# Full fp32 products on unsplit operands in the mixing phases of a decoder trunk

## The chip, the cores and the metric

The kernel runs on one core of one Trainium2 chip. The metric is the device time of one execution in microseconds (us); less is better. Times of two kernels are compared from runs on the same chip.

## The reference

Two layers (`DEPTH = 2`) work on 256 tokens of 1024 features in fp32. Each layer is a half-step feed-forward, a mixing part and a second half-step feed-forward. The mixing part joins two groups of heads, sparse attention and a gated linear recurrence (HGRN2):

```python
for l in range(DEPTH):
    x = x + 0.5 * swiglu(rmsnorm(x, ffn1_norm[l]), ffn1_w_gate[l], ffn1_w_up[l], ffn1_w_down[l])
    h = rmsnorm(x, mix_norm[l])
    proj = h @ w_in[l]
    (q, kc, vc, ksl, vsl, kw, vw, gts, hq, hf, hi, hg) = jnp.split(proj, offsets, axis=-1)
    ...
    o_nsa = nsa_group(...)      # 8 heads of 64, 2 key groups, three branches
    o_hg = hgrn2_group(...)     # 4 heads of 128
    x = x + jnp.concatenate([o_nsa, o_hg], axis=-1) @ w_out[l]
    x = x + 0.5 * swiglu(rmsnorm(x, ffn2_norm[l]), ffn2_w_gate[l], ffn2_w_up[l], ffn2_w_down[l])
```

In the attention each head has three softmaxes, over compressed blocks, selected blocks and a window; their outputs, weighted by gates, are added:

```python
o_s = jnp.einsum("bgrqnl,bgqnld->bqgrd", p2.astype(dt), vg)
o_w = jnp.einsum("bgrqk,bkgd->bqgrd", p3.astype(dt), vwb)
o = gb[..., 0:1] * o_c + gb[..., 1:2] * o_s + gb[..., 2:3] * o_w
```

With 256 tokens the selected blocks are all blocks and the window holds every earlier token, so both branches are causal attention over the whole sequence.

## The kernel before

The tokens stand as two halves of 128, h = 0 and 1. The weights come as a stream of units of 512 KB, in one order for the whole program, phase by phase: feed-forward, mixing, feed-forward, twice. A unit holds two K tiles of 128 rows by 512 columns. `load_stream` (L373) loads each into one of three raw buffers (`raw`, fp32); `hi_stream` (L391) rounds it to fp32r on ScalarE into `hi` of one of five ring slots; `lo_stream` (L410) subtracts, on VectorE or GpSimd, to give `lo`, and then frees the raw buffer. The activations are split in the same way (`split`, L363): a rounded part on ScalarE, the rest on VectorE. A product of two split operands is three fp32r matmuls, hi hi, hi lo and lo hi (L463 to L465; L493 to L495 where the weights are the stationary operand). `stream` (L436) issues the products of one half; a ring slot is free when both halves have used its unit.

A mixing phase has input products (`w_in`, 24 full units and 4 narrower ones), then 8 units of output weights (`w_out`) in `OUT_ORDER`: part 0 multiplies the attention's outputs for both halves of the columns, part 1 the recurrence's. Beside the stream run tasks for the attention (`attend_task`, L1082, with `head_task`, `turn_task` and `cmp_task`) and for the recurrence (`level_task`, `products`, `out_task`). `turn_task` (L1172) transposes 128 keys of four heads' probabilities into PSUM and splits them into `pth` and `ptl`; `pv` (L1118) multiplies them by the values `vh` and `vl`, which stand between columns of zeros (`pad`, L561). The attention's output is split into `ah` and `al` (L1140), the recurrence's into the activations' tiles `XH` and `XL` (L1411), which is why it waits for the end of the input products (L1409).

The order of instructions on each engine is made when the program is built: `Sched.run` (L193) takes, of all tasks, the operation that could start first by costs that the program holds for each kind of operation, plus a penalty per task (`PEN`); where several engines could run it, it takes the one that would end first. `stream_pen` (L509) holds the second half back in the last `LAG = 4` units of a phase until the first half is done, so that the first half's norm (`resid`, `norm`, `norm_turn`, L650 to L682) can run beside the second half's products. All transfers are issued by SyncE's queue, in one order.

Of the kernel before, what the change touches and what calls it, by code (L numbers as in the profile page):

```python
# [25 lines left out]
LARGE = 85.0   # the exponential of more could overflow  # L26
LEVELS = [0, 1, 2, 4, 8, 16, 32]

# columns of the constant array
# [9 lines left out]
# moving layout of the keys of a group: sel 1 | sel 0 | win 0 | win 1 | compressed  # L39
# [5 lines left out]
RING = 5       # split weight units held  # L45
RAW = 3        # unsplit weight units held
BOOT = 3       # units split by K tiles at the start
# when the rest of the inputs is loaded: after which unit of weights, half, from and to which 256 columns
BOOT_X = ((-1, 0, 1, 2), (0, 0, 2, 4), (2, 1, 0, 2), (3, 1, 2, 4))
FIRST = (-0.3, -0.4, 0.5, 1.3, 0.1, 0.6, 0.9, 0.2)  # L50
LAG = 4        # units by which the halves of the tokens are apart at a phase's ends
NBUF = 14      # general buffers of the mixing part
# [3 lines left out]
# how eager the tasks are (less: earlier)  # L56
# [43 lines left out]
class Op:  # L100
    """An instruction (or a few for one engine), with the engines that could run it, each with what it costs there."""
# [15 lines left out]
LOAD = 1.28    # a switch of ScalarE's tables  # L117
# [4 lines left out]
class Sched:  # L122
    """Emits the instructions of tasks that run side by side, in the order in which they could start.

    A task is a generator. It yields an Op (and is sent the op's end), or a request: wait for a key
    or a condition, set a key, acquire a slot (sent the slot), release it. An op waits for what its
    task has waited for or done before."""
# [26 lines left out]
    def resolve(self, t):  # L154
        """A request that isn't an op; whether it could be met."""
        what, arg = t.req[0], t.req[1]
        if what == "wait":
            if callable(arg):
                if not arg():
                    return False  # L160
            elif arg not in self.keys:
                return False
            else:
                t.deps += self.keys[arg]
            self.advance(t)
        elif what == "deps":
            t.deps = list(arg)
            self.advance(t)
        elif what == "set":
            self.keys[arg] = list(t.deps)  # L170
            self.advance(t)
        elif what == "acq":
            have = self.slots[arg]
            n = t.req[2]
            if len(have) < n:
                return False
            have.sort(key=lambda x: max((d[0] for d in x[1]), default=0.0))
            got = [have.pop(0) for _ in range(n)]
            self.last_acq = [y for _, d in got for y in d]
            t.deps += self.last_acq  # L180
            self.advance(t, [x for x, _ in got])
        elif what == "rel":
            for x in t.req[2]:
                self.slots[arg].append((x, list(t.deps)))
            self.advance(t)
        return True
# [6 lines left out]
    def run(self):  # L193
        while self.tasks:
# [29 lines left out]
            if eng == "DMA":  # L224
                # its issue, then the transfer, which others hold up
                issued = end - cost + 0.475
                self.moved = max(issued + 0.65, self.moved) + cost
                end = self.moved + 0.87
# [7 lines left out]
def four(t):  # L236
    """Two K tiles of 512 columns as four of 256."""
    return t.rearrange("p a (b n) -> p (a b) n", b=2)
# [29 lines left out]
class Block:  # L268
    """Columns of a product that share an accumulator: [128 tokens, n] for each half, or, where the weights are the
    stationary operand, [128 columns, 2, 256 tokens]."""  # L270
# [5 lines left out]
class Unit:  # L276
    """1024 x 128 of a block's weights: two K tiles of 512 columns, or four of 256."""

    def __init__(self, block, kt, srcs, first, last, act, need):
        self.block, self.kt, self.srcs = block, kt, srcs  # L280
        self.first, self.last, self.act, self.need = first, last, act, need


class Trunk(Sched):
# [33 lines left out]
    def copy(self, out, in_, after=None):  # L318
        """A copy, by either of two engines."""
# [36 lines left out]
    def transposes(self, pairs):  # L356
        """pairs: (out, in)."""
# [9 lines left out]
    def rope_norm(self, st, n):  # L367
        """st [128, 2, n]: sums of squares in, inverse norms out, both in the first row."""
# [22 lines left out]
    def hi_stream(self):  # L391
        for i, u in enumerate(self.units):
            self.at_hi = i
            if i >= BOOT:
                yield wait(("raw", i))
            (s,) = yield acq("ring")
# [13 lines left out]
    def lo_stream(self):  # L410
        for i, u in enumerate(self.units):
# [12 lines left out]
            yield wait(("hi", i))  # L424
            hi, lo = self.split_w[i]
# [10 lines left out]
    def stream(self, h):  # L436
        for p, (a, b) in enumerate(self.phases):
            self.phase_at[h] = p
            for i in range(a, b):
# [19 lines left out]
                def mm(t):  # L459
                    ah, al = u.act(h, u.kt + t)  # L460
                    st, sp = u.first and t == 0, u.last and t == 1
                    f = self.nc.tensor.matmul
                    f(ps[:, :k.n], ah, hi[:, t, :k.n], start=st, stop=False)  # L463
# [3 lines left out]
                for t in range(2):  # L467
                    if i < BOOT:
                        yield wait(("lo", i, t))
                    yield self.P(3 * (0.0025 + k.n / 2400), lambda: mm(t))  # L470
                self.used[i] = self.used.get(i, 0) + 1
                if self.used[i] == 2:
                    yield rel("ring", self.split_w.pop(i))
# [51 lines left out]
    def control(self):  # L525
        """One phase's memory after the other's."""
# [8 lines left out]
    def start(self):  # L535
# [14 lines left out]
        self.padded = [per.tile([128, 4, 320], F32R, name=n) for n in ("vh", "vl")]  # L550
# [10 lines left out]
    def pad(self):  # L561
        """Zeros that stay, of what only in part takes data."""
        nc = self.nc
        vh, vl, gv, vcb = self.padded
        for t in [gv, vcb] + self.pcs:
            yield self.G(0.25, lambda: nc.gpsimd.memset(t, 0.0))
        z = vcb[:, 0:1, 0, :64].to_broadcast([128, 4, 64])
        for v in (vh, vl):
            for o in (0, 128, 256):
                yield self.G(0.97, lambda: nc.gpsimd.tensor_copy(v[:, :, o:o + 64], z))  # L570
        yield put("padded")

    def boot(self):
        """What the start waits for, in the order in which it is needed."""
# [34 lines left out]
    def first_turn(self, h, n):  # L609
        """The first product starts before the norm is known: of the inputs times the gains, transposed."""  # L610
# [47 lines left out]
    def norm(self, h, i):  # L658
        """The i-th norm of the half h: its transposed, split activations."""
# [179 lines left out]
    def mix(self, l):  # L839
# [3 lines left out]
        M = {}  # L843
# [65 lines left out]
        def values(h, br, src):  # L909
            """src [128, g, 64] -> split, between columns of zeros."""  # L910
            c = lambda v: v[:, 2 * br + h, 64:].rearrange("p (g d) -> p g d", g=2)[:, :, :64]
            yield from self.split(c(M["vh"]), c(M["vl"]), src)
# [169 lines left out]
        def attend_task(h, g):  # L1082
# [3 lines left out]
            # the heads' segments: branch, where in the scores, width, mask  # L1086
# [21 lines left out]
            vh, vl, vcb = M["vh"], M["vl"], M["vcb"]  # L1108
# [4 lines left out]
            for i, (so, vi) in enumerate(tiles):  # L1113
                yield wait(key("pt", h, g, i))
                yield wait(key("v", vi % 2, vi // 2))
                th, tl = M["pt", h, g, i]

                def pv(e):  # L1118
                    o = 64 + 128 * g - 64 * e
                    c = slice(256 * e, 256 * e + 256)  # L1120
                    f = nc.tensor.matmul
                    f(po[:, :256], vh[:, vi, o:o + 128], th[:, c], start=(i == 0 and e == 0), stop=False)
                    f(po[:, :256], vl[:, vi, o:o + 128], th[:, c], start=False, stop=False)
                    f(po[:, :256], vh[:, vi, o:o + 128], tl[:, c], start=False, stop=False)

                for e in range(2):
                    yield P(0.33, lambda: pv(e))
                yield rel("pth", (th, tl))
# [11 lines left out]
            yield from self.split(M["ah", h][:, s], M["al", h][:, s], po[:, :256].rearrange("p (k t) -> p k t", k=2))  # L1140
# [3 lines left out]
        def head_task(h, g, r, part, pr, mx):  # L1144
            """One head's probabilities, weighted by the gates of their branches."""
# [26 lines left out]
        def turn_task(h, g, i, so, pr):  # L1172
            (pt,) = yield acq("short")
            yield self.transposes([(pt[:, 128 * k:128 * k + 128], pr[r][:, so:so + 128]) for k, r in enumerate((0, 2, 1, 3))])
            ((th, tl),) = yield acq("pth")
            yield from self.split(th, tl, pt)
            M["pt", h, g, i] = th, tl
# [3 lines left out]
        def cmp_task(h, g):  # L1181
            """The probabilities of the compressed branch, transposed."""
# [40 lines left out]
        def f_task(c, ps):  # L1223
            """The forget gates of two heads, transposed."""
# [101 lines left out]
        def products(h, i, a, b, x):  # L1326
            """A level's products within 64 tokens: for its right halves alone, but for the diagonal."""
# [28 lines left out]
        def last_product(h, x):  # L1356
# [9 lines left out]
            # what is no longer needed holds the whole matrix  # L1366
# [11 lines left out]
        def out_task(h):  # L1378
# [30 lines left out]
            yield wait(lambda: self.phase_done_in(h))  # L1409
            c = slice(128 * h, 128 * h + 128)  # L1410
            yield from self.split(self.XH[:, 4:8, c], self.XL[:, 4:8, c], h4(pt))  # L1411
# [18 lines left out]
        act = lambda h, kt: self.xact(h, kt) if kt > 3 else (M["ah", h][:, kt], M["al", h][:, kt])  # L1430
        for ni, (part, n) in enumerate(OUT_ORDER):
            for k in (2 * part, 2 * part + 1):
# [3 lines left out]
                us.append(Unit(bs[n], 2 * k, [(wo[256 * k:256 * k + 256, 512 * n:512 * n + 512], 0)], first, last, act, need))  # L1436

        def opened(pool, p):
# [3 lines left out]
            self.slots["hx"] = [(T([128, 512], f"hx{i}"), []) for i in range(4)]  # L1442
            self.slots["pth"] = [((T([128, 512], f"pth{i}", F32R), T([128, 512], f"ptl{i}", F32R)), []) for i in range(2)]
# [8 lines left out]
            for h in range(2):  # L1452
                M["ah", h], M["al", h] = T([128, 4, 128], f"ah{h}", F32R), T([128, 4, 128], f"al{h}", F32R)
# [11 lines left out]
            M["vh"], M["vl"], M["gv"], M["vcb"] = self.padded  # L1465
# [64 lines left out]
```

## Time and profile before

| what | value |
|---|---|
| median of 3 runs | 1146.16 us (1146.1 to 1149.26) |
| span of the profiled execution | 1147.0 us; the page gives no other time of it |
| TensorE (PE) busy | 1080.8 us, 94% |
| VectorE (DVE) busy | 720.7 us, 63% |
| ScalarE (ACT) busy | 571.7 us, 50% |
| GpSimd (POOL) busy | 200.5 us, 17% |
| mean granted TensorE clock | 0.976 |
| the chain that ended last | PE 75%, DVE 16%, issue 4%, DMA 2% |

The busy shares are means over the whole span. The feed-forwards make up most of it, and TensorE is busy there almost throughout; the mixing phases lie at about 211 to 391 us and 773 to 954 us and look different, so they are read by stretches. PEld is the load of stationary operands and runs beside PE. A matmul's duration holds its latency; what the engine needs for one is the step from its start to the next one's start.

### The profile page before, as it was taken

How to read it: one execution, taken by the hardware profiler on the slowest of the kernel's cores; microseconds unless marked ns; L12 is line 12 of the kernel's file. 1: busy time of each engine (PE TensorE's matmuls, PEld its weight loads, DVE VectorE, ACT ScalarE, POOL GpSimd, SP SyncE). 2: the span in 40 equal slices, each digit the busy share in tenths (PEclk: the TensorE clock that was granted, in tenths of full speed). 3: DMA queues.
4: the chain of work that ended last, by engine and by line, in shares of the span. 5: the costliest groups of instructions: out<-in, count | busy, mean ns of one | idle time of the engine just before them, and what ended most of it. 6: DMA issues, size and time to landing. Idle time of an engine off the chain costs nothing.

```text
span 1147.0 us, 18786 instructions
## 1 busy us (share of the span) xinstructions
PE 1080.8 (94%) x7420; PEld 974.6 (85%) x7420; DVE 720.7 (63%) x1187; ACT 571.7 (50%) x899; POOL 200.5 (17%) x193
## 2 busy tenths in 40 slices
PE   5999999988879999999999999999898799999998
PEld 4999988777668799998879999877876688999986
DVE  5565544777998665554465555447889976655543
ACT  5554444465756554444354444434675555444432
POOL 2200000353554200000020000013635622000000
PEclk9999999998989999999999999999998899999999
DMA  7666655564313476666666666555551235766553
GB/s 220 197 188 194 188 185 185 148 167 129 110 55 93 147 200 187 184 185 184 188 171 199 187 178 190 181 161 160 144 167 56 74 110 145 204 184 183 183 157 121
DMA packets 154168, 186.16 MB, mean 162 GB/s; under 512 B 7568, under 2 KB 117984, under 8 KB 154080
## 3 DMA queue, kind: packets, MB, share of 16 engines
q1 hardware_dynamic: 154080, 184.96, 54.7%
q8 instruction: 58, 0.95, 0.3%
q14 instruction: 30, 0.25, 0.1%
HBM read 183.89 MB, written 1.05 MB: 161 GB/s over the span
## 4 chain that ended last, share of the span: by engine, by line
PE 75%; DVE 16%; issue 4%; DMA 2%; ACT 1%; POOL 1%; SPq 1%; DVEq 0%; POOLq 0%; ACTq 0%
PE acc L493 14%; PE acc L494 14%; PE acc L495 14%; PE acc L463 9%; PE acc L465 9%; PE acc L464 9%; DVE buf L326 2%; PE short L360 2%; DVE lo L326 2%; DVE xn L668 1%; DVE buf L1156 1%; DVE hx L326 1%; DVE kk L336 1%; DVE P L326 1%; DVE ptl L326 1%
## 5 line engine op out<-in xcount | busy, mean ns | idle before, releaser
L326 DVE TENSOR_TENSOR lo<-raw,hi 128x1024 fp32r<-128x1024 f32 (+2 forms) x302 | 365.6, 1214 | 286.5 <-ACT hi L313 285.5
L313 ACT ACTIVATE hi<-raw 128x1024 fp32r<-128x1024 f32 (+2 forms) x337 | 350.6, 1043 | 309.2 <-PE acc L465 110.8
L493 PE MATMUL acc<-xh,hi 128*128 128x256 f32 x1408 | 402.4, 286 | 0.0
L494 PE MATMUL acc<-xl,hi 128*128 128x256 f32 x1408 | 401.1, 285 | 0.0
L495 PE MATMUL acc<-xh,lo 128*128 128x256 f32 x1408 | 400.9, 285 | 0.0
L493 PEld LDWEIGHTS acc<-xh,hi 128*128 128x128 f32 x1408 | 273.2, 194 | 0.2
L494 PEld LDWEIGHTS acc<-xl,hi 128*128 128x128 f32 x1408 | 273.1, 194 | 0.1
L495 PEld LDWEIGHTS acc<-xh,lo 128*128 128x128 f32 x1408 | 273.0, 194 | 0.0
L463 PE MATMUL acc<-hi,th 128*128 128x512 f32 x352 | 139.5, 396 | 0.0
L464 PE MATMUL acc<-lo,th 128*128 128x512 f32 x352 | 139.2, 395 | 0.0
L465 PE MATMUL acc<-hi,tl 128*128 128x512 f32 x352 | 139.1, 395 | 0.0
L354 POOL TENSOR_TENSOR rs<-rs,half 128x1 f32<-128x1 f32 x12 | 7.0, 587 | 552.2 <-DVE rs L661 552.2
L328 POOL TENSOR_TENSOR lo<-raw,hi 128x1024 fp32r<-128x1024 f32 (+1 forms) x37 | 89.4, 2422 | 68.6 <-ACT hi L313 43.2
L463 PE MATMUL acc<-hi,xh 128*128 128x512 f32 (+1 forms) x240 | 98.6, 411 | 0.0
L465 PE MATMUL acc<-hi,xl 128*128 128x512 f32 (+1 forms) x240 | 93.0, 387 | 0.0
L464 PE MATMUL acc<-lo,xh 128*128 128x512 f32 (+1 forms) x240 | 92.7, 386 | 0.0
L465 PEld LDWEIGHTS acc<-hi,tl 128*128 128x128 f32 x352 | 66.1, 188 | 16.1
L463 PEld LDWEIGHTS acc<-hi,th 128*128 128x128 f32 x352 | 66.2, 188 | 15.6
L464 PEld LDWEIGHTS acc<-lo,th 128*128 128x128 f32 x352 | 66.1, 188 | 15.6
L313 ACT ACTIVATE sg<-acc 128x512 f32<-128x512 f32 (+1 forms) x46 | 26.1, 568 | 66.8 <-PE acc L495 64.4
L465 PEld LDWEIGHTS acc<-hi,xl 128*128 128x128 f32 x240 | 46.2, 193 | 9.3
L463 PEld LDWEIGHTS acc<-hi,xh 128*128 128x128 f32 x240 | 46.8, 195 | 6.8
(233 smaller groups left out, 1174.9 us busy)
## 6 DMA issues: line engine op xcount, KB each, us to landing
raw<-in_ffn_w_down_dram SPq DMA_DIRECT2D x88, 512.0 KB, 4.0
raw<-in_ffn_w_gate_dram SPq DMA_DIRECT2D x80, 512.0 KB, 3.8
raw<-in_ffn_w_up_dram SPq DMA_DIRECT2D x80, 512.0 KB, 4.1
raw<-in_w_in_dram SPq DMA_DIRECT2D x48, 512.0 KB, 3.7
raw<-in_w_out_dram SPq DMA_DIRECT2D x16, 512.0 KB, 3.8
buf<-in_cmp_w_dram SPq DMA_DIRECT2D x16, 256.0 KB, 5.1
raw<-in_ffn_w_gate_dram SPq DMA_DIRECT2D x13, 256.0 KB, 2.8
raw<-in_ffn_w_up_dram SPq DMA_DIRECT2D x13, 256.0 KB, 3.1
```

What stands on the lines that cost most here:

```text
L313: return ("ACT", c, lambda: self.nc.scalar.activation(out, in_, func, **k), TABLES.get(func))
L326: alts = [("DVE", 0.065 + 0.00104 * n, lambda: self.nc.vector.tensor_tensor(out, a, b, op), None)]
L328: alts.append(("POOL", 0.13 + 0.00213 * n, lambda: self.nc.gpsimd.tensor_tensor(out, a, b, op), None))
L336: lambda: self.nc.vector.tensor_scalar(out, a, s1, s2, **k), None)]
L360: self.nc.tensor.transpose(o, i, self.ident[:i.shape[0], :i.shape[0]])
L463: f(ps[:, :k.n], ah, hi[:, t, :k.n], start=st, stop=False)
L464: f(ps[:, :k.n], ah, lo[:, t, :k.n], start=False, stop=False)
L465: f(ps[:, :k.n], al, hi[:, t, :k.n], start=False, stop=sp)
L493: f(ps[:, c], hi[:, t, j], xh, start=u.first and c == t == 0, stop=False)
L494: f(ps[:, c], hi[:, t, j], xl, start=False, stop=False)
L495: f(ps[:, c], lo[:, t, j], xh, start=False, stop=u.last and c == 1 and t == 3)
L668: toks.append((yield self.V(576, lambda: nc.vector.scalar_tensor_tensor(self.XN[h][:, c], self.X[h][:, c], rs[:, 0:1], self.gains[0][:, c] ...
```

## The change

Unsplit fp32 operands replace split ones in two products of the mixing phase, and their splits go. A matmul of two fp32 operands is one call in place of three.

- Probabilities times values: `turn_task` copies the transposed probabilities into an fp32 tile (`pf`, two buffers of its own), the values are one fp32 tile (`vh`), `pv` is one matmul.
- Output products: the attention's output is an fp32 tile `ah`, the recurrence's an fp32 tile of its own, `oh`, so that `out_task` no longer waits for the end of the input products. Units of output weights are marked `whole`: they get no ring slot and no split, are used from the raw buffer, and free it when both halves have used it.
- The zeros beside the values are written by fills in place of copies. The scheduler's cost of a whole product is four matmuls where it was three.

The core of the diff (other lines that change are comments and docstrings):

```diff
@@ hi_stream, lo_stream, stream @@
+            if u.whole:
+                self.split_w[i] = self.raw.pop(i), None
+                yield put(("hi", i))
+                continue
             (s,) = yield acq("ring")
...
+            if u.whole:
+                yield put(("lo", i))
+                continue
             hi, lo = self.split_w[i]
...
+                    if u.whole:
+                        f(ps[:, :k.n], ah, hi[:, t, :k.n], start=st, stop=sp)
+                        return
                     f(ps[:, :k.n], ah, hi[:, t, :k.n], start=st, stop=False)
...
-                    yield self.P(3 * (0.0025 + k.n / 2400), lambda: mm(t))
+                    yield self.P((4 if u.whole else 3) * (0.0025 + k.n / 2400), lambda: mm(t))
                 self.used[i] = self.used.get(i, 0) + 1
                 if self.used[i] == 2:
-                    yield rel("ring", self.split_w.pop(i))
+                    x = self.split_w.pop(i)
+                    if u.whole:
+                        yield rel("raw", x[0])
+                    else:
+                        yield rel("ring", x)
@@ start, pad @@
-        self.padded = [per.tile([128, 4, 320], F32R, name=n) for n in ("vh", "vl")]
+        self.padded = [per.tile([128, 4, 320], F32, name="vh")]
...
-        z = vcb[:, 0:1, 0, :64].to_broadcast([128, 4, 64])
-        for v in (vh, vl):
-            for o in (0, 128, 256):
-                yield self.G(0.97, lambda: nc.gpsimd.tensor_copy(v[:, :, o:o + 64], z))
+        for o in (0, 128, 256):
+            yield self.G(0.4, lambda: nc.gpsimd.memset(v[:, :, o:o + 64], 0.0))
@@ mix @@
-            c = lambda v: v[:, 2 * br + h, 64:].rearrange("p (g d) -> p g d", g=2)[:, :, :64]
-            yield from self.split(c(M["vh"]), c(M["vl"]), src)
+            yield self.copy(M["vh"][:, 2 * br + h, 64:].rearrange("p (g d) -> p g d", g=2)[:, :, :64], src)
...
-                    f(po[:, :256], vh[:, vi, o:o + 128], th[:, c], start=(i == 0 and e == 0), stop=False)
-                    f(po[:, :256], vl[:, vi, o:o + 128], th[:, c], start=False, stop=False)
-                    f(po[:, :256], vh[:, vi, o:o + 128], tl[:, c], start=False, stop=False)
+                    nc.tensor.matmul(po[:, :256], vh[:, vi, o:o + 128], th[:, c], start=(i == 0 and e == 0), stop=False)
...
-                    yield P(0.33, lambda: pv(e))
-                yield rel("pth", (th, tl))
+                    yield P(0.45, lambda: pv(e))
+                yield rel("pf", th)
...
-            yield from self.split(M["ah", h][:, s], M["al", h][:, s], po[:, :256].rearrange("p (k t) -> p k t", k=2))
+            yield self.copy(M["ah", h][:, s], po[:, :256].rearrange("p (k t) -> p k t", k=2))
...
-            ((th, tl),) = yield acq("pth")
-            yield from self.split(th, tl, pt)
-            M["pt", h, g, i] = th, tl
+            (th,) = yield acq("pf")
+            yield self.copy(th, pt)
+            M["pt", h, g, i] = th
...
-            yield wait(lambda: self.phase_done_in(h))
-            c = slice(128 * h, 128 * h + 128)
-            yield from self.split(self.XH[:, 4:8, c], self.XL[:, 4:8, c], h4(pt))
+            yield self.copy(M["oh", h], h4(pt))
...
-        act = lambda h, kt: self.xact(h, kt) if kt > 3 else (M["ah", h][:, kt], M["al", h][:, kt])
+        act = lambda h, kt: (M["oh", h][:, kt - 4] if kt > 3 else M["ah", h][:, kt], None)
...
+            self.slots["pf"] = [(T([128, 512], f"pf{i}"), []) for i in range(2)]
```

## Rows read from the trace of the kernel before

**Rows 1.** The page: busy us, share and instructions of each engine.
```profile
PE 1080.8 (94%) x7420; PEld 974.6 (85%) x7420; DVE 720.7 (63%) x1187; ACT 571.7 (50%) x899; POOL 200.5 (17%) x193
```

**Rows 2.** Busy us by stretch (length, engines, granted clock, DMA share, GB/s).
```profile
285.00:320.00 35.00, 29.22 (x254) 22.56 (x250) 32.75 (x146) 24.56 (x81) 19.46 (x23) 0.95 0.37 105
320.00:362.00 42.00, 35.91 (x327) 30.94 (x328) 38.84 (x101) 27.07 (x60) 23.18 (x21) 0.88 0.26 76
362.00:391.00 29.00, 27.77 (x145) 23.14 (x144) 21.16 (x26) 15.27 (x22) 9.28 (x8) 1.00 0.37 108
846.00:881.00 35.00, 29.91 (x244) 23.16 (x244) 32.26 (x146) 24.18 (x79) 19.57 (x23) 0.90 0.36 102
881.00:925.00 44.00, 36.61 (x328) 31.39 (x329) 40.79 (x102) 26.98 (x60) 23.18 (x21) 0.88 0.24 73
```

**Rows 3.** Timeline of VectorE, 333 to 359 us: start, us, line, operation.
```profile
333.25 2.58 DVE L326 TENSOR_TENSOR hx<-hx,xn 128x256 f32<-128x256 f32 x1
...
336.73 2.45 DVE L326 TENSOR_TENSOR P<-P 128x256 f32<-128x256 f32 x1
...
350.29 1.38 DVE L326 TENSOR_TENSOR hx<-hx,kk 128x256 f32<-128x256 f32 x1
351.60 0.41 DVE L326 TENSOR_TENSOR hx<-hx,xn 128x256 f32<-128x256 f32 x1
...
353.92 2.58 DVE L326 TENSOR_TENSOR hx<-hx,kk 128x256 f32<-128x256 f32 x1
...
357.08 1.27 DVE L326 TENSOR_TENSOR ptl<-short,pth 128x512 fp32r<-128x512 f32 x2
```

**Rows 4.** Timeline of GpSimd, the first of four such splits.
```profile
333.21 2.35 POOL L328 TENSOR_TENSOR lo<-raw,hi 128x1024 fp32r<-128x1024 f32 x1
```

**Rows 5.** The chain of waits from 320 to 362 us: start, us, what.
```profile
329.92 1.20 DVE ptl L326 x2
...
333.32 2.51 DVE hx L326
...
336.73 2.45 DVE P L326
...
350.39 1.61 DVE hx L326 x2
```

**Rows 6.** Timeline of TensorE: start, us, line, operation, idle time before it.
```profile
347.67 0.28 PE L1122 MATMUL po<-pth,vh 128*128 128x256 f32 x1
...
348.01 0.28 PE L1122 MATMUL po<-pth,vh 128*128 128x256 f32 x1
...
362.17 0.40 PE L463 MATMUL acc<-hi,ah 128*128 128x512 f32 x1
...
362.87 0.40 PE L463 MATMUL acc<-hi,ah 128*128 128x512 f32 x1
...
372.79 0.38 PE L1397 MATMUL po<-xn,S 128*128 128x128 f32 x2
...
374.34 0.39 PE L1399 MATMUL po<-xn,xn 128*128 128x128 f32 x2
...
390.62 0.66 PE L360 MATMUL short<-ident,xn 128*128 128x128 f32 x4 [1.23 <-DVE xn L668]
```

**Rows 7.** The page: transfers of output weights, KB each, us to landing.
```profile
raw<-in_w_out_dram SPq DMA_DIRECT2D x16, 512.0 KB, 3.8
```

**Rows 8.** Timeline of VectorE at the mixing phase's end.
```profile
383.52 0.69 DVE L653 SCALAR_TENSOR_TENSOR x<-acc,x 128x512 f32<-128x512 f32 x1 [1.53 <-PE acc L465]
...
386.56 1.22 DVE L326 TENSOR_TENSOR lo<-raw,hi 128x1024 fp32r<-128x1024 f32 x1
387.69 2.88 DVE L668 SCALAR_TENSOR_TENSOR xn<-x,rs,gain 128x512 f32<-128x512 f32 x1
```

**Rows 9.** Timeline of ScalarE: the first and the last attention output, of four.
```profile
326.60 0.38 ACT L313 ACTIVATE ah<-po 128x256 fp32r<-128x256 f32 x1
...
359.71 0.39 ACT L313 ACTIVATE ah<-po 128x256 fp32r<-128x256 f32 x1 [0.19 <-PE po L1136]
```

More of the change, by code (lines that the diff above doesn't have):

```diff
@@ L276, with __init__ @@
 class Unit:
-    def __init__(self, block, kt, srcs, first, last, act, need):
-        self.block, self.kt, self.srcs = block, kt, srcs
+    def __init__(self, block, kt, srcs, first, last, act, need, whole=False):
+        self.block, self.kt, self.srcs, self.whole = block, kt, srcs, whole
         self.first, self.last, self.act, self.need = first, last, act, need
@@ L563, in pad @@
         nc = self.nc
-        vh, vl, gv, vcb = self.padded
+        v, gv, vcb = self.padded
         for t in [gv, vcb] + self.pcs:
             yield self.G(0.25, lambda: nc.gpsimd.memset(t, 0.0))
-        z = vcb[:, 0:1, 0, :64].to_broadcast([128, 4, 64])
-        for v in (vh, vl):
-            for o in (0, 128, 256):
-                yield self.G(0.97, lambda: nc.gpsimd.tensor_copy(v[:, :, o:o + 64], z))
+        for o in (0, 128, 256):
+            yield self.G(0.4, lambda: nc.gpsimd.memset(v[:, :, o:o + 64], 0.0))
         yield put("padded")
@@ L1107, in attend_task @@
             (po,) = yield acq("po")
-            vh, vl, vcb = M["vh"], M["vl"], M["vcb"]
+            vh, vcb = M["vh"], M["vcb"]
             yield put(key("po", *tag))
@@ L1115, in attend_task @@
                 yield wait(key("v", vi % 2, vi // 2))
-                th, tl = M["pt", h, g, i]
+                th = M["pt", h, g, i]
                 def pv(e):
@@ L1120, in pv @@
                     c = slice(256 * e, 256 * e + 256)
-                    f = nc.tensor.matmul
-                    f(po[:, :256], vh[:, vi, o:o + 128], th[:, c], start=(i == 0 and e == 0), stop=False)
-                    f(po[:, :256], vl[:, vi, o:o + 128], th[:, c], start=False, stop=False)
-                    f(po[:, :256], vh[:, vi, o:o + 128], tl[:, c], start=False, stop=False)
+                    nc.tensor.matmul(po[:, :256], vh[:, vi, o:o + 128], th[:, c], start=(i == 0 and e == 0), stop=False)
                 for e in range(2):
-                    yield P(0.33, lambda: pv(e))
-                yield rel("pth", (th, tl))
+                    yield P(0.45, lambda: pv(e))
+                yield rel("pf", th)
             yield rel("buf", *bufs)
@@ L1435, in mix @@
                 last = k == 2 * part + 1 and part == OUT_ORDER[-1][0]
-                us.append(Unit(bs[n], 2 * k, [(wo[256 * k:256 * k + 256, 512 * n:512 * n + 512], 0)], first, last, act, need))
+                us.append(Unit(bs[n], 2 * k, [(wo[256 * k:256 * k + 256, 512 * n:512 * n + 512], 0)], first, last, act, need, True))
         def opened(pool, p):
@@ L1452, in opened @@
             for h in range(2):
-                M["ah", h], M["al", h] = T([128, 4, 128], f"ah{h}", F32R), T([128, 4, 128], f"al{h}", F32R)
+                M["ah", h], M["oh", h] = T([128, 4, 128], f"ah{h}"), T([128, 4, 128], f"oh{h}")
                 M["qs", h] = T([128, H, 128], f"qs{h}", F32R)
@@ L1463, in opened @@
             M["ax"] = M["Q", 1]
-            M["vh"], M["vl"], M["gv"], M["vcb"] = self.padded
+            M["vh"], M["gv"], M["vcb"] = self.padded
             self.slots["pc"] = [(x, []) for x in self.pcs]
```

## The prediction

> **What bounds the kernel now.** I read the page first. TensorE is busy 94% of the span [rows 1], so over most of it nothing but fewer columns could help. The change touches the two mixing phases alone, so next come the busy times by stretch around them [rows 2]. The reader is to see three regimes in each layer. From 285 to 320 VectorE is busy 32.75 of 35 us. From 320 to 362 it is busy 38.84 of 42, while TensorE has 35.91 at a granted clock of 0.88. From 362 to 391 TensorE has 27.77 of 29 at 1.00 and VectorE, with 21.16, has room. The second layer repeats this at 846, 881 and 925. So the middle stretch waits for VectorE and the last one for TensorE: work taken from VectorE is worth something in the one, work given to TensorE costs in full in the other.
>
> The timelines of VectorE and GpSimd show why VectorE is so full [rows 3, 4]. A multiplication of 128x256 takes 0.41 us at 351.60, but 2.58 at 333.25 and 353.92, 1.38 at 350.29, and an addition 2.45 at 336.73: each time GpSimd has just begun the split `lo` of a unit of the output weights, as at 333.21; there are four of them, one for each long operation. The chain of waits goes through long ones and through the `ptl` splits [rows 5].
>
> **The change, part by part.** The sum is made against the profiled span of 1147.0 us; that is 0.84 above the median of the runs, 1146.16, so 0.84 comes off at the end.
>
> *Output products.* Each layer has 8 units of output weights, 2 halves and 2 K tiles: 32 products of 512 columns. Today each is three matmuls; the next product starts 0.70 us after the first (362.17 to 362.87) [rows 6]. No row shows an fp32 product of 512 columns. The nearest are the HGRN products, fp32 on both sides with 128 columns: each stands as two records, and from the first start at 372.79 to the last at 374.34 there are seven steps, 0.221 us each [rows 6]. A record of fp32 with 128 columns (0.111) thus costs what one of fp32r with 256 does (0.34/3 = 0.113, from 347.67 to 348.01): a column costs double in each of two records, which excludes that the whole form gets cheaper. In proportion 512 columns take 0.886, that is +0.186, times 64 = **+11.9 us**. High end: four times the step of an fp32r matmul of 512 columns (0.233) is 0.933, +14.9. Low end: if a tenth of the 0.111 didn't grow with the columns, it would be 2 x (0.011 + 0.4) = 0.82, +7.8. I take proportion. In the last stretch nothing hides it.
>
> The Trainium skill (FP8 and Floating Point Precision, TensorE Precision Notes) says that true fp32 takes four passes through the array; by that and the step above the sum would hold 14.9 in place of 11.9 and the time would be 3 us longer. The rows of 128 columns lie a little under it, 0.221 against a quarter of 0.933.
>
> *Probabilities times values.* Six tiles for each of two groups, two matmuls of 256 columns per tile: 24 a layer. Today three matmuls take 0.34; in fp32 2 x 0.221 = 0.44: +0.10 x 48 = **+4.8 us** of TensorE (3.2 with the low price, 6.0 with the high one). It lies in the middle stretch and counts as far as that gets TensorE-bound.
>
> *Splits taken away.* In the middle stretch VectorE loses the excess of the four long operations (2.17 + 2.04 + 0.97 + 2.17 = 7.3 us), ten `ptl` at 0.60 (1.27 for two) = 6.1 [rows 3], and four `al` at 0.33. That is 14.7 of 38.84, so VectorE no longer binds there. What TensorE has to do then sets the limit: its busy time at full clock is 35.91 x 0.88 = 31.6 and 36.61 x 0.88 = 32.2, so the slack of the two stretches is 10.4 + 11.8 = 22.2 us [rows 2]. How much of it comes back? On the chain itself stand 1.20 us of `ptl` and the excess of three long operations, 2.17 + 2.11 + 0.93 (their pieces of 2.51, 2.45 and 1.61, the last of two operations, less 0.34 for each) [rows 5]: 6.4 us a layer. Six smaller pieces like them are left out of the sum, because another chain lies close behind (the levels of the recurrence, and TensorE's transposes). I take the 6.4: **-12.8 us**. Ends: 8.6 (only the two longest stalls) and 22.2.
> ScalarE's `hi` of the output weights go as well; it is busy 27.07 of 42, and nothing waits for it there: nothing. The fp32 copies of values and of outputs replace halves of splits that are done now: nothing. The pad's casts become fills at the start, where the chain is in loads: nothing. The HGRN outputs no longer wait for the end of the input products; the output products of part 0 cover that wait today: nothing.
>
> *Weights that stay in the raw buffers.* There are three, and each is free only when both halves have used its unit; today a unit leaves the raw buffer after its split and five more lie in the ring. The load of output unit 3 now waits for TensorE's second half on unit 0, and behind it on SyncE's queue wait the other output units, the next feed-forward's weights and its gain. While products follow each other this is hidden: a unit lasts 4 x 0.886 = 3.5 us, a load 3.8 [rows 7], with two units in between. It is not hidden at the end of the phase. Today the first half runs ahead (its last residual starts at 383.52) [rows 8], and the second half's products cover its norm, so that TensorE idles only 1.23 us before the last transposes of it at 390.62 [rows 6]. With three buffers unit 7 can only be loaded once the second half is through unit 4 (time T). It lands near T + 4.0, the first half needs 1.8 for it, and the norm up to its last transposes another 7.1 us as now (383.52 to 390.62), or 3.7 without the `lo` of 1.22 at 386.56 and the 2.2 by which `xn` at 387.69 is longer than an operation of that width (2.88 against 0.69 at 383.52) [rows 6, 8]. That is T + 9.5 to 12.9, against 7.1 us of products left (four half-units of 1.77). TensorE idles 2.4 to 5.8; less today's 1.2 that is 1.2 to 4.6. I take 3.0 a layer, about the middle, **+6.0 us**; ends 2.4 and 9.2. The ring is empty then too; the loads for the first units start as the last output units free their buffers, under the norm.
>
> The sum: 1147.0 + 11.9 + 4.8 - 12.8 + 6.0 = 1156.9, less 0.84: **1156.1 us**.
>
> **Rivals.**
> *The relief wins (faster).* One mechanism: without the stalls the middle stretch gets TensorE-bound and gives back all its slack, 22.2 us, and the stretch before it, with slack of 35 - 29.22 x 0.95 = 7.2 and 35 - 29.91 x 0.90 = 8.1, a third, 5. For it: VectorE loses a good third of its work in the middle. Against it: in the stretch from 285 to 320 only two `ptl` go, and TensorE's idle time is also waits in chains. 1156.1 + 12.8 - 27.2 = 1141.7; with the pause at its low end 1138. It decides from some 23 us given back (11.9 + 4.8 + 6.0).
> *A wash.* The stretch gives back 20 us, or 16 with no longer pause: 1156.1 - 7.2 = 1149, or 1156.1 - 3.2 - 6.0 = 1147. For it: VectorE falls from nine tenths to under six in the middle. Against: the added 16.7 us of columns are sure.
> *Three buffers starve TensorE (slower still).* The second half's attention is ready late (its last `ah` at 359.71, the first half's first at 326.60) [rows 9]; the first half can go ahead by three units only and nothing fills the middle. 8.6 given back, the pause at 4.6 a layer, and after it a fall to the lower of TensorE's two clock levels, 1.2 of 2.4 GHz, as in the idling middle stretch, which at 0.88 loses 0.12 x 42 = 5 us by it; 2 a layer here, an estimate from that: 1156.1 + 4.2 + 3.2 + 4 = 1167.5.
>
> **How the numbers follow.** Chances: the forecast 0.50, starving 0.13, a wash 0.15, the relief 0.22. A measurement tells about 0.3% from no change, 3.4 us. Faster by more: the relief, 0.22. Within: the wash, 0.15. Slower: the forecast and starving, 0.63. The forecast's own range, with two or three of its costs towards their ends, is 1150 to 1163; so that no more than 2 in 10 is left out, the range reaches through most of the relief and to starving: 1140 to 1168.
>
> **What would show each step.** The output products stand as two records each, 0.886 us from one product to the next; 0.82 or 0.93 tells an end. The VectorE operations of 2.5 us beside a GpSimd `lo` are gone between the last input weights' split and the output products, and VectorE is busy there well under nine tenths. That stretch is some 4 us shorter a layer (6.4 less 2.4 for the values); if TensorE still idles for VectorE there, the relief was overrated, if it is shorter by 8 or more, underrated. Before the second feed-forward's first product TensorE idles 4 us or more, released by VectorE's norm, with a late load of the last output unit before it; without that pause the step on the buffers is wrong. An order of instructions that shifts outside the mixing phases would make the whole sum wrong, since it takes the other 900 us as they are.

## The result and the profile after

The changed kernel takes 1195.03 us in the median of four runs (1193.09 to 1199.32), the kernel before 1146.63 beside it: a ratio of 1.0423, 95% interval 1.0394 to 1.0453. That is slower, by some 48 us, and 27 us above the upper end of the predicted range.

The page of the changed kernel, against [rows 1]: VectorE, ScalarE and GpSimd lose work as meant; TensorE gains 35.1 us.

```profile
PE 1115.9 (94%) x7308; PEld 968.8 (81%) x7308; DVE 687.4 (58%) x1159; ACT 554.5 (47%) x873; POOL 157.5 (13%) x166
```

Busy times by stretch of the changed kernel, with the columns of [rows 2]; the phase now ends some 20 us later, so a stretch is added.

```profile
285.00:320.00 35.00, 28.96 (x278) 20.58 (x277) 28.53 (x54) 15.22 (x31) 18.70 (x18) 0.95 0.21 62
320.00:362.00 42.00, 33.36 (x196) 24.65 (x196) 32.36 (x185) 24.98 (x90) 2.39 (x12) 0.80 0.19 51
362.00:391.00 29.00, 29.00 (x131) 18.82 (x130) 4.48 (x8) 7.63 (x14) 2.04 (x2) 1.00 0.22 63
391.00:411.00 20.00, 13.57 (x37) 5.72 (x36) 8.63 (x11) 6.93 (x13) 3.43 (x3) 0.95 0.46 145
```

The middle stretch, which was to gain, has TensorE at 33.36 us and a clock of 0.80, where it had 35.91 and 0.88 [rows 2]. Behind it TensorE is full for 29 us while VectorE works 4.48 of them and GpSimd 2.04. Work that stood side by side now stands one after the other. That points to the order, not to a price.

TensorE's timeline has the longer products, two records each, at about the prices foretold. From 385.00 to 388.54 are four of 512 columns, 0.885 us each; the next four take 3.60, and less the 1.02 of one that stands alone, over three steps, that is 0.86. The probabilities' 14 records are seven matmuls of 256 columns; from their start to that of the next instruction, at 370.73, they take 3.17 us, 0.45 each.

```profile
367.56 3.34 PE L1132 MATMUL po<-pf,vh 128*128 128x256 f32 x14
370.73 0.61 PE L1144 MATMUL po<-pct,vcb 128*128 128x128 f32 x4
...
377.51 1.02 PE L471 MATMUL acc<-raw,ah 128*128 128x512 f32 x2
...
385.00 3.70 PE L471 MATMUL acc<-raw,ah 128*128 128x512 f32 x8
388.54 3.60 PE L471 MATMUL acc<-raw,oh 128*128 128x512 f32 x8
```

Now the order. In the kernel before, VectorE's timeline shows the last of the four value splits of this phase at 286.08, 39 us after the third:

```profile
246.77 0.29 DVE L326 TENSOR_TENSOR vl<-acc,vh 128x128 fp32r<-128x128 f32 x1 [0.47 <-ACT vh L313]
286.08 0.28 DVE L326 TENSOR_TENSOR vl<-acc,vh 128x128 fp32r<-128x128 f32 x1
```

and TensorE's the transposes of the keys (eight, both halves), on which all scores wait, with two of the attention's scores four microseconds on:

```profile
282.94 1.03 PE L360 MATMUL short<-ident,buf 128*128 128x128 f32 x8
...
286.73 0.39 PE L1152 MATMUL short<-kh,qs 128*128 128x256 f32 x1
286.95 0.28 PE L1153 MATMUL short<-kl,qs 128*128 128x256 f32 x1
```

In the changed kernel the last value copy on VectorE ends at 245, and the transposes come at 320.51, 38 us later than before; until then TensorE had input products and the recurrence's levels. The two timelines, VectorE's and then TensorE's:

```profile
244.71 0.28 DVE L322 COPY vh<-acc 128x128 f32<-128x128 f32 x1
```

```profile
320.51 1.03 PE L360 MATMUL short<-ident,buf 128*128 128x128 f32 x8
```

The code says how the one could bring the other. The order is made when the program is built. `k_turn` and the stream of a half that is behind have the same penalty, 0.15 (`PEN`, `FLOW[1]`), and a tie goes to the stream, which is earlier in the list. In the kernel before the stream of the second half could not take its turn, since an accumulator that it needed for its next input product still held the keys and values whose low part was to be split off. With one copy in place of the split the accumulator is free early, the stream has its turn, and the transposes wait until input products and levels are through. The delay of the transposes, and of the attention behind them, is called the slip below. This is the order theory. Its rival, the cost theory, is that the full fp32 products and the three raw buffers themselves cost 48 us and the order came along with them.

### The profile page after: what moved, and what is told of

Same layout as the page of the kernel before. It is cut to its first block, busy times and chain, and to the rows that moved or that the text cites. A ratio compares the mean times of both kernels' runs of the same rounds, so it can differ in the third digit from the quotient of the medians.

```text
span 1191.3 us, 18448 instructions
## 1 busy us (share of the span) xinstructions
PE 1115.9 (94%) x7308; PEld 968.8 (81%) x7308; DVE 687.4 (58%) x1159; ACT 554.5 (47%) x873; POOL 157.5 (13%) x166
## 4 chain that ended last, share of the span: by engine, by line
PE 77%; DVE 14%; DMA 4%; ACT 2%; issue 2%; POOL 1%; SPq 0%; DVEq 0%; POOLq 0%; ACTq 0%
PE acc L507 13%; PE acc L508 13%; PE acc L509 13%; PE acc L473 9%; PE acc L474 9%; PE acc L475 9%; PE acc L471 4%; PE short L360 3%; DVE buf L326 2%; DVE lo L326 2%; DVE hx L326 2%; PE po L1132 2%; DVE xn L680 1%; DVE buf L1164 1%; DMA raw<-in_ffn_w_gate_dram 1%
## 5 line engine op out<-in xcount | busy, mean ns | idle before, releaser
L313 ACT ACTIVATE hi<-raw 128x1024 fp32r<-128x1024 f32 (+2 forms) x321 | 334.0, 1044 | 309.2 <-PE acc L475 104.0
L473 PE MATMUL acc<-hi,xh 128*128 128x512 f32 (+1 forms) x208 | 86.2, 414 | 0.0
L474 PE MATMUL acc<-lo,xh 128*128 128x512 f32 (+1 forms) x208 | 80.5, 387 | 0.0
L475 PE MATMUL acc<-hi,xl 128*128 128x512 f32 (+1 forms) x208 | 80.1, 385 | 0.0
L473 PEld LDWEIGHTS acc<-hi,th 128*128 128x128 f32 x352 | 66.2, 188 | 15.6
L328 POOL TENSOR_TENSOR lo<-raw,hi 128x1024 fp32r<-128x1024 f32 (+1 forms) x23 | 55.9, 2433 | 31.1 <-ACT hi L313 31.1
L326 DVE TENSOR_TENSOR sg<-acc,sg 128x512 f32<-128x512 f32 (+1 forms) x46 | 30.1, 657 | 32.6 <-PE acc L509 29.2
L475 PEld LDWEIGHTS acc<-hi,xl 128*128 128x128 f32 x208 | 40.5, 195 | 7.9
```

Source lines behind the costliest of these rows:

```text
L313: return ("ACT", c, lambda: self.nc.scalar.activation(out, in_, func, **k), TABLES.get(func))
L326: alts = [("DVE", 0.065 + 0.00104 * n, lambda: self.nc.vector.tensor_tensor(out, a, b, op), None)]
L328: alts.append(("POOL", 0.13 + 0.00213 * n, lambda: self.nc.gpsimd.tensor_tensor(out, a, b, op), None))
L474: f(ps[:, :k.n], ah, lo[:, t, :k.n], start=False, stop=False)
L475: f(ps[:, :k.n], al, hi[:, t, :k.n], start=False, stop=sp)
```

## The experiments

Each was timed beside the kernel before on the same chip; differences in us are the ratio's share of its 1148 to 1149 us. But for the two that say so, the builder made the order anew for each, so small shifts elsewhere are in their numbers.

**The accumulator held.** The whole change and one wait:

```diff
+            if h:
+                yield wait(key("k", h))
             yield from values(h, 0, p4[:, 3])
             yield rel(f"acc{h}", ps)
```

> The whole change, with one wait added: the accumulator that holds the keys and values of the second half is let go only when the keys of that half have been transposed, about as late as the value splits let it go before. Order theory (the unsplit values let the accumulator go some 40 us earlier, the second half's input products run ahead of the keys' transposes, and the attention slips behind the recurrence's levels): the keys' transposes come back to about 283 us of the first mixing phase, and what is left are the steps of the prediction, 11.9 + 4.8 + 6.0 less a relief between 0 and 12.8, so 1147 to 1170 us, 25 us or more under the changed kernel. Cost theory (full fp32 products and three unsplit buffers cost that much more than the sum had, and the order came along with them): 1180 us or more.

Measured: 1159.73 us, ratio 1.0089 (1.0065 to 1.0113), +10.2 us. TensorE's timeline has the transposes back:

```profile
281.61 1.03 PE L360 MATMUL short<-ident,buf 128*128 128x128 f32 x8
```

So 38 of the 48 us (48.5 by the ratio, less 10.2) were the order, and the cost theory falls.

**The slip alone.** The kernel before with `"k_turn": 0.35` in place of 0.15.

> The kernel before, with nothing of the change, but the keys' transposes (k_turn) less eager, 0.35 where 0.15 stood, so that the input products and the levels go ahead of them on TensorE. Order theory: the slip alone costs some 15 to 21 us a layer, so 1176 to 1188 us. Cost theory: the order is worth little, within 8 us of 1146.6 us.

Measured: 1187.06 us, 1.0329 (1.0291 to 1.0367), +37.8 us. Nothing of the change is in it; the slip by itself costs about what the held accumulator gave back. The transposes come nine microseconds later still than in the changed kernel:

```profile
329.57 1.03 PE L360 MATMUL short<-ident,buf 128*128 128x128 f32 x8
```

**The accumulator let go early.** The kernel before with `"kv_task": 0.0` in place of 0.65.

> The kernel before, with all its splits, but with the task that copies the keys and values out of the accumulator made more eager (kv_task, 0.0 where 0.65 stood), so that the last value split is made early and the accumulator of the second half let go some 40 us sooner. Nothing else is changed, and the keys' transposes keep their 0.15. Order theory, with the accumulator as the trigger: the same slip as in the run with less eager transposes, +30 to +42 us, 1179 to 1191 us. Rival (the accumulator is not what holds the second half's input products, the unsplit values set off the slip in another way): within 8 us of the kernel before.

Measured: 1177.27 us, 1.0255 (1.0216 to 1.0295), +29.3 us, just under the range expected. The trigger is shown: with every split in place, the last value split at 247.41 sends the transposes to 321.65. Timelines of VectorE, of TensorE, and the middle stretch:

```profile
247.41 0.29 DVE L326 TENSOR_TENSOR vl<-acc,vh 128x128 fp32r<-128x128 f32 x1 [0.47 <-ACT vh L313]
```

```profile
321.65 1.03 PE L360 MATMUL short<-ident,buf 128*128 128x128 f32 x8
```

```profile
320.00:362.00 42.00, 32.68 (x204) 25.18 (x202) 35.31 (x193) 28.74 (x98) 6.01 (x11) 0.76 0.28 81
```

The stretch looks as in the changed kernel: TensorE at 32.68 (there 33.36), its clock at 0.76 (0.80).

**The tie broken.** The whole change with `"k_turn": 0.14`.

> The whole change as it is, but for the keys' transposes' penalty, 0.14 where 0.15 stood, which breaks its tie with the input products in the transposes' favour. Order theory: the attention no longer slips, 1150 to 1172 us. Cost theory: 1185 us or more.

Measured: 1155.84 us, 1.0060 (1.0042 to 1.0077), +6.9 us. One hundredth in a penalty is worth some 42 us here (48.5 less 6.9). It does not bring back the order of the kernel before: the keys' transposes now come ahead of it, a half at a time, each together with four others, at 256.69 and 270.10 in place of 282.94.

```profile
256.69 1.97 PE L360 MATMUL short<-ident,buf 128*128 128x128 f32 x8 [2.78 <-DVE buf L322]
...
270.10 1.07 PE L360 MATMUL short<-ident,buf 128*128 128x128 f32 x8 [1.69 <-DVE buf L322]
```

**Each part alone.** Probabilities times values in fp32 with the output products split as before, and the reverse.

> Probabilities times values in full fp32 on unsplit operands alone; the output products, their activations and their weights are split as before. It holds the values' single copy, so by the order theory it slips like the whole change: 1146.6 + 30 to 42 for the slip + 4.8 for the products less a few for the splits, 1172 to 1192 us. Cost theory: 4.8 us less some of the splits' relief, 1143 to 1152 us.

> Output products in full fp32 on unsplit activations and weights alone; values and probabilities are split as before, and so the accumulator is held as before. Order theory: no slip, the steps of the output part alone, 11.9 + 6.0 less a relief between 0 and 9, so 1155 to 1165 us. Cost theory: most of the changed kernel's loss is here, 1180 to 1195 us.

Measured: 1173.82 us, 1.0212 (1.0184 to 1.0240), for the first, 1160.90, 1.0099 (1.0077 to 1.0122), for the second. The part that copies the values slips, the one that keeps their splits doesn't; the keys' transposes in the first and in the second:

```profile
324.70 1.03 PE L360 MATMUL short<-ident,buf 128*128 128x128 f32 x8
```

```profile
282.29 1.03 PE L360 MATMUL short<-ident,buf 128*128 128x128 f32 x8
```

**Probabilities times values with the accumulator held.**

> Probabilities times values in full fp32 on unsplit operands, with the accumulator of the second half's keys and values held until the keys are transposed; the output products as before. By the prediction's steps: +4.8 for the 48 longer products less the part of the relief that is the probabilities' and values' (their splits are most of what stalled in the mixing phase), so 1140 to 1150 us. Rival (the splits' stalls are hidden, and only the longer products count): 1151 to 1154 us.

Measured: 1142.33 us, 0.9944 (0.9929 to 0.9958), -6.4 us: against 4.8 of longer products, if they count in full, 11.2 us of relief from splits of 128x512 probabilities and of values. A part of it is TensorE's clock, at 1.00 in the middle stretch, where it had 0.88 [rows 2]:

```profile
320.00:362.00 42.00, 37.58 (x357) 30.77 (x356) 35.14 (x90) 28.70 (x67) 18.39 (x25) 1.00 0.21 65
```

**Output weights in more buffers.** The whole change with the accumulator held; units 3 to 7 go to general buffers of the mixing part (`NRAW = 3`):

```diff
+            if u.whole and i - self.in_end >= NRAW:
+                yield wait(self.bufs_free)
+                pair = yield acq("buf", 2)
...
+                for j in range(2):
+                    yield self.dma(pair[j], ap[128 * j:128 * j + 128], 1 << 18)
```

> The whole change with the accumulator held, and units 3 to 7 of each layer's output weights loaded into pairs of the mixing part's general buffers, as soon as the four attention parts have theirs, so that no output unit waits for a raw buffer. Pause theory (the three raw buffers cost what TensorE waits at the end of the phase, in the run with the accumulator held 6.5 us in each layer: 0.43 + 1.22 for the weights, 1.97 + 2.86 for the norms): 10 to 13 us under that run, 1146 to 1151 us. Rival (the norms at the phase's end are late for another reason, as the stream has one half close behind the other anyway): only the waits for the weights go, 2 to 4 us, 1155 to 1158 us.

Measured: 1142.40 us, 0.9938 (0.9921 to 0.9955). Three raw buffers cost 10.2 + 7.1 = 17.3 us, give or take some 3, more than the pause theory had. With three, and the accumulator held, TensorE waits at the phase's end; its timeline:

```profile
377.40 6.28 PE L471 MATMUL acc<-raw,oh 128*128 128x512 f32 x14 [0.43 <-DMA raw<-in_w_out_dram]
384.89 4.56 PE L471 MATMUL acc<-raw,oh 128*128 128x512 f32 x10 [1.22 <-DMA raw<-in_w_out_dram]
391.42 1.37 PE L360 MATMUL short<-ident,xn 128*128 128x128 f32 x8 [1.97 <-DVE xn L680]
395.66 1.11 PE L360 MATMUL short<-ident,xn 128*128 128x128 f32 x4 [2.86 <-DVE xn L680]
396.42 0.77 PE L473 MATMUL acc<-hi,xh 128*128 128x512 f32 x1
397.00 0.63 PE L474 MATMUL acc<-lo,xh 128*128 128x512 f32 x1
397.42 0.63 PE L475 MATMUL acc<-hi,xl 128*128 128x512 f32 x1
397.85 0.63 PE L473 MATMUL acc<-hi,xh 128*128 128x512 f32 x1
```

After the waits the clock is low as well: by stretch 0.76 and 0.56, then 1.00 again.

```profile
390.00:395.00 5.00, 1.37 (x8) 0.84 (x8) 4.26 (x5) 3.83 (x6) 3.38 (x3) 0.76 0.81 252
395.00:400.00 5.00, 4.34 (x16) 3.61 (x17) 4.26 (x6) 1.65 (x3) 1.62 (x2) 0.56 0.34 79
400.00:405.00 5.00, 5.00 (x24) 4.09 (x23) 0.99 (x2) 1.55 (x2) 1.52 (x1) 1.00 0.99 315
```

The waits are 6.48 us a layer; the lower level takes, by estimate, another 1.37 x 0.24 + 4.34 x 0.44 = 2.2. Twice 8.7 is 17.4, which accounts for the measured price. Of the last wait, 2.86, some 2 us are one VectorE operation of the second half's norm, 2.83 us long beside a GpSimd split; the first half's two took 1.41 together. VectorE's timeline, then GpSimd's:

```profile
390.62 1.41 DVE L680 SCALAR_TENSOR_TENSOR xn<-x,rs,gain 128x512 f32<-128x512 f32 x2
...
392.77 2.83 DVE L680 SCALAR_TENSOR_TENSOR xn<-x,rs,gain 128x512 f32<-128x512 f32 x1 [0.67 <-POOL rs L354]
```

```profile
392.71 2.35 POOL L328 TENSOR_TENSOR lo<-raw,hi 128x1024 fp32r<-128x1024 f32 x1
```

With the general buffers the first half's norm lies beside products again, and TensorE's timeline names no wait there:

```profile
384.33 0.60 PE L361 MATMUL short<-ident,xn 128*128 128x128 f32 x4
384.77 1.02 PE L482 MATMUL acc<-buf,oh 128*128 128x512 f32 x2
385.63 0.60 PE L361 MATMUL short<-ident,xn 128*128 128x128 f32 x4
386.07 2.74 PE L482 MATMUL acc<-buf,oh 128*128 128x512 f32 x6
```

The middle stretch of this run, to set against [rows 2]:

```profile
320.00:362.00 42.00, 40.30 (x360) 31.25 (x359) 29.11 (x87) 24.27 (x63) 13.12 (x20) 1.00 0.27 89
```

**The output part with these buffers.**

> Output products in full fp32 alone (values and probabilities split as before), with units 3 to 7 of the output weights in pairs of general buffers. Against the same part with three raw buffers (+12.0 us) it gives the pause: by the pause theory 15 to 18 us less, 1143 to 1147 us, since the pause was 17 us in the whole change. If in the whole change the general buffers gained by something that has to do with the probabilities: 5 to 10 us less, 1151 to 1156 us.

Measured: 1144.88 us, 0.9963 (0.9948 to 0.9978), -4.2 us. Against +11.4 with three buffers (1.0099) the pause is 15.6 here: the same thing without the probabilities.

**A fourth product.** The kernel before with `f(ps[:, :k.n], al, lo[:, t, :k.n], start=False, stop=False)` added to each output product; the builder's costs, and so the order, stay.

> The kernel before with one more product in each of the 64 output products, the low part of the activations times the low part of the weights, so that TensorE does 0.233 us more in each and nothing else changes. If the output products lie wholly on the path, as the prediction's +11.9 took them: 64 x 0.233 = +14.9 us, 1161 to 1164 us. If part of them is hidden by the phase's stalls: 1149 to 1158 us.

Measured: 1162.26 us, 1.0110 (1.0094 to 1.0125), +12.6 us of 14.9. TensorE's time in the output products lies on the path for the most part, about 85% by the middle of the interval (72 to 97% by its ends).

**Without the low parts' splits.** The kernel before, with `lambda: None` issued in place of the subtraction for the 16 output units; the order stays.

> The kernel before without the 16 subtractions that split the low parts of the output weights, eight on GpSimd in the middle stretches and eight on VectorE behind them; the products that read them stay and read what the buffers held. It leaves out the low part of the output weights, and nothing else is changed, the order of the instructions neither. By the prediction's step, the excess of the three long VectorE operations that stood on the chain comes back, 2.17 + 2.11 + 0.93 = 5.2 us a layer: -10.4, 1136 to 1140 us. If the relief that the runs gave (some 14 us for the output part) is mostly GpSimd's stalls: 1131 to 1135 us. If those stalls are hidden behind the splits of the probabilities, which stay here: 1142 to 1148 us.

Measured: 1139.43 us, 0.9912 (0.9889 to 0.9934), -10.1 us, inside the range that the prediction's step gave. The middle stretch:

```profile
320.00:362.00 42.00, 39.51 (x346) 34.28 (x346) 35.68 (x101) 29.75 (x64) 14.16 (x17) 0.88 0.26 81
```

TensorE gains 3.6 us in it and the clock nothing.

The stalls that went are not all those of the step. A GpSimd split and a long VectorE operation beside it stand here too, where [rows 4] and [rows 3] have them at 333.21 and 333.25; GpSimd's timeline, then VectorE's:

```profile
332.46 2.35 POOL L329 TENSOR_TENSOR lo<-raw,hi 128x1024 fp32r<-128x1024 f32 x1
```

```profile
332.50 2.58 DVE L327 TENSOR_TENSOR hx<-hx,xn 128x256 f32<-128x256 f32 x1
```

Only the splits of output weights are left out, so this one is of the last input unit, and [rows 4] is not the first of the four. Of the three pieces on the chain 2.17 us stay, and 2.11 + 0.93 = 3.0 a layer can go, 6.1 in all if the second layer is as the first. The two traces say much the same. From the queries' last transposes to those of the first half's norm at the phase's end it is 151.11 us before (239.51 to 390.62 [rows 6]) and 148.37 here; in the second layer 151.72 and 148.62. That is 2.7 + 3.1 = 5.8 us. TensorE's timelines, before and here:

```profile
239.51 0.46 PE L898 MATMUL short<-identr,ptl 128*128 128x128 f32 x4
```

```profile
238.61 0.46 PE L902 MATMUL short<-identr,ptl 128*128 128x128 f32 x4
...
386.98 0.66 PE L361 MATMUL short<-ident,xn 128*128 128x128 f32 x4 [1.23 <-DVE xn L672]
```

The times show more, 7.6 to 12.8 us by the interval, and the two profiled spans differ by 7.0; where the rest of the 10.1 comes from stays open.

**Both mends.** The whole change, the tie broken by 0.14, and the general buffers.

> The whole change with the tie broken by the transposes' penalty 0.14 and units 3 to 7 of the output weights in pairs of general buffers: the version that the runs so far point to. If the two gains add (0.9938 with the accumulator held; the broken tie was 3 us better than that hold), 1138 to 1143 us; if the earlier transposes only gained what the general buffers now give, 1143 to 1147 us.

Measured: 1141.10 us, 0.9930 (0.9907 to 0.9954). It beats both kernels, by some 8 us and some 56; from the version with the accumulator held and the same buffers (0.9938) it can't be told apart. In full the two gains would give 0.9909, which the interval holds as well, so whether they add stays open.

## Why the prediction was wrong

**The step that failed** is the sentence that the fp32 copies of values and outputs "replace halves of splits that are done now: nothing". In its own time the copy of the values costs nothing: 0.28 us, as the last value split took on VectorE alone. But it ends the hold on an accumulator some 40 us earlier; that hold had kept the second half's input products behind the keys' transposes, and its end cost 38 us (48.5 less 10.2; 37.8 with the slip alone, 29.3 with the early split alone). The prediction had named an order that shifts as what would undo the sum, but outside the mixing phases; it shifted within them, where the text took the order of the trace of before as given.

**The sum without the slip.** The prediction gave 9.9 us over the profiled span; with the order held the change costs 10.2. That is luck and not a sum that came right: two terms were far off and made up for each other.

- *Output products, +11.9.* The price of one was right (0.86 to 0.885 against 0.886). By the fourth product's 85% some 10 of it reach the end. The four passes that the Trainium skill gives (FP8 and Floating Point Precision, TensorE Precision Notes) would be 0.933, an estimate by that page; the rows lie 5 to 8% under it, and they decide.
- *Probabilities times values, +4.8.* 0.45 against 0.44: right (the low end, 3.2, should be 3.9 by the text's own low price).
- *Splits taken away, -12.8.* Too small, and in part for a stall that stays. With 10.1 + 4.8 paid and 7.1 won, the relief is 22.0 us, an estimate from these runs, at the end (22.2) that the text worked out from TensorE's slack. The text took the split at 333.21 for one of the output weights; it is of the last input unit, and so 2.17 us a layer of the 5.2 that stood for stalls do not go with the output splits. What these give is 5.8 us by the traces and 10.1 by the times, with 10.4 in the sum: that the times come near it does not show the step right. The larger miss is in what was left out since "another chain lies close behind": the probabilities' and values' part alone gave 11.2, where the sum had 2.4; which of its pieces gave how much was not taken apart. With both kinds gone TensorE does 40.30 us at full clock in the middle stretch, where it did 35.91 x 0.88 = 31.6 [rows 2]. The parts don't add (-6.4 and -4.2 alone, -7.1 together), as it would be if the second relief found part of the slack used; that was not tested.
- *The pause, +6.0.* Too small, 17.3 measured and 9.2 the upper end. Its mechanism was right: a late last load, then a norm that nothing covers. It was sized as the wait for one norm less today's 1.23 [rows 6]; both norms were waited for, 1.97 + 2.86, the weights before them, 0.43 + 1.22, and the clock fell after that, which the text had only in the rival in which TensorE starves.

**The rivals.** None named the order. The relief wins once the order is held and the pause taken away (0.9938).

That the slip costs so much is seen in the stretches: with the attention behind the levels, VectorE's work on scores meets TensorE idle (33.36 of 42, clock 0.80) and TensorE's fp32 products meet VectorE idle (4.48 of 29). How the 38 us divide between idle time and clock was not taken apart.

## What to carry to other kernels

Where a scheduler makes the order, an edit's first price is the order that it makes: a buffer that comes free sooner is a change of its own, and ties between penalties are where it tips. Set the two orders side by side, engine by engine, before pricing terms, and ask which task was kept waiting by what the edit shortens. When weights are used where they were loaded, count the buffers that the lag between two consumers needs at a phase's end, not those that a steady stream needs. If several chains are relieved at once, bound the gain by the slack of the engine that then binds.

## What the runs showed of the hardware

An fp32 product of 512 columns takes 0.86 to 0.885 us in two records, a little under four times an fp32r step of 0.233.

In the run with the accumulator held TensorE's granted clock was at 1.00 for 60 us, short waits of 0.43 and 1.22 among them. Then came waits of 1.97 and 2.86 us with 1.37 us of work between them, and the clock of the next two stretches of 5 us was 0.76 and 0.56. In the second a matmul of 512 columns took a step of 0.43 us (397.42 to 397.85), the lower level of 1.2 GHz, in place of 0.23. The stretch ahead of them:

```profile
330.00:390.00 60.00, 57.61 (x347) 37.05 (x343) 27.01 (x59) 22.05 (x47) 10.04 (x14) 1.00 0.20 58
```

VectorE operations that take 0.41 us took 1.38 to 2.58 beside a GpSimd split [rows 3]. In the run without the output weights' splits the operations on the same tiles between 330 and 358 us take 0.41 to 0.87, but for the one of 2.58 at 332.50, beside the split that stayed.
